# Second branch's attention outputs loaded between the late gates, and two staging tiles for those gates

## The chip, the cores and the metric

The kernel runs on one core of a Trainium2 chip. The metric is device time in microseconds (us) of one execution, the median of several runs. TensorE (PE in the profile) does the matrix products into PSUM, the accumulator memory of eight banks; VectorE (DVE), ScalarE (ACT) and GpSimd (POOL) do the elementwise work; SyncE's queue (SP) issues nearly all DMAs. Every engine works off its own instructions in the order in which they were written, and waits for other engines by semaphores.

## The reference, cut to what matters

One layer over 1040 positions (16 meta tokens and 1024 frames) of width 1024, in float32. Two attention branches of eight heads each share one input projection; their outputs are projected, gated and added:

```python
    log_keep = jnp.where(causal, jax.nn.log_sigmoid(-z), 0.0)
    later = lax.cumsum(log_keep, axis=3, reverse=True) - log_keep
    a = jnp.where(causal, jnp.exp(jax.nn.log_sigmoid(z) + later), 0.0)   # second branch
...
    y_a = _merge_heads(o_a) @ w_o_fox[layer]
    y_b = _merge_heads(o_b) @ w_o_sb[layer]
    mixed = (jax.nn.sigmoid(g_a) * y_a + jax.nn.sigmoid(g_b) * y_b) @ w_out[layer]
```

g_a and g_b, the gates, are 2 x 1024 columns of the input projection. A norm, a residual, a convolutional feed-forward part and a second residual follow; the change doesn't touch them.

## The kernel before, in words

Activations stand with channels on the 128 partitions. Every float32 product is made of three float32r products (a high and a low part of each operand), so 8 blocks of the contraction give 24 matmuls for one output tile (`products`, L133). The 1040 positions are cut in three pieces, `PCS`, of 272, 384 and 384.

Attention goes through 16 heads, x = 0 to 15, branch b = 0 then b = 1. For a head, `attention` walks four chunks c of two query blocks. In the second branch a query block is: scores `s` on PE (L360, L361, L363), two sigmoids on ACT into `kp` and `pr` (L393, L394), a reverse running product `kp` on DVE (L411), a product `pr` on POOL (L412), transposes `tm` and `tr` on PE (L422, L432), casts on ACT and subtractions on DVE that split them into `ptm` and `pt` (L424, L425, L436, L437), and the weighted sum `po` on PE (L426, L442). `ot` and `os` (L445, L447) add its two halves, and a DMA (L448) writes them to `od`, a DRAM tensor for every branch and pair of heads. Between heads `prep(x + 1)` makes the queries, keys and values of the next head (`pq`, `pv`).

`gate(x)` makes one of 16 blocks of 128 gate columns: three tiles `pg` on PE (one for each piece: 24 matmuls 258 wide, twice 24 matmuls 384 wide), in the two PSUM banks of tag "lin"; DVE scales them into a staging tile `gst` in SBUF (L498), where pieces 0 and 1 share one tile and piece 2 has its own; DMAs write the tiles to `gd` in DRAM (L500). Gates 0 to 8 are called inside the loop over the heads, behind the heads of the same numbers. The last seven (`LATE = 7`) are called behind the whole attention stage: the variable x of that loop names gates 9 to 15, whose column blocks i are 12, 5, 13, 6, 14, 7, 15 (a tile `pg120` is block 12, piece 0).

Behind attention comes the output stage: `oraw` tiles (128x258) are loaded from `od` (L571), 32 of them, and split by ACT and DVE into `o` tiles (L572, L573); `gate_load` reads gates back into `gs` and applies the sigmoid; and for eight blocks `y` is multiplied out of them on PE and gated by DVE (L602).

Two things set the order of an engine's work. The program is written in the order told here, and a scheduler with a model of the engines' times orders it by priority as soon as an instruction's operands and its tile's place are to be had. Tiles come from pools. `xp` lives from the start through the late gates. `ga` is opened behind the attention stage, whose pools have then been closed; a tile in a place that an attention tile had waits until that tile's last user is done.

Of the kernel before, what the change touches and what calls it, by code (L numbers as in the profile page):

```python
# [8 lines left out]
F32 = mybir.dt.float32  # L9
F32R = mybir.dt.float32r  # L10
# [6 lines left out]
P = 128  # L17
# [4 lines left out]
L = NM + NX  # L22
A0 = 14
# [21 lines left out]
PCS = [(0, 272), (272, 656), (656, L)]  # L45
QS = [(a, a + QW) for a in range(0, NX, 256)]
# [3 lines left out]
def block_kernel(ctx, tc, xa, xb, wqk, wv, wf, bfg, wg, wo, wout, wup, wdn, gains, conv, cst, out):  # L50
    nc = tc.nc

    def f(ap):
        return ap.bitcast(F32)
# [34 lines left out]
    def sub(eng, dst, a, hi):  # L89
        eng.tensor_tensor(dst, a, f(hi), op=ALU.subtract)  # L90
# [21 lines left out]
    def load_w(src, n, what, eng=None, into=None, hv=False, behind=(None, None)):  # L112
        raw = wp.tile([P, KT * P], F32, tag="wraw", bufs=3, name=f"wr_{what}")
        nc.sync.dma_start(raw[:, :n], src)
        hi, lo = into or (wp.tile([P, KT * P], F32R, tag="whi", name=f"wh_{what}"),
                          wp.tile([P, KT * P], F32R, tag="wlo", name=f"wl_{what}"))
        if hv:
            nc.vector.tensor_copy(hi[:, :n], raw[:, :n])
        else:
            with after(behind[0]):  # L120
                nc.scalar.copy(hi[:, :n], raw[:, :n])  # L121
        with after(behind[1]):
            sub(eng or nc.gpsimd, lo[:, :n], raw[:, :n], hi[:, :n])
        return hi, lo
# [3 lines left out]
    def products(ps, hi, lo, xs, k0, k1, n0, n1, waits=(None,) * 3):  # L128
        xh, xl = xs
        for s, (w, x) in enumerate(((hi, xh), (hi, xl), (lo, xh))):  # L130
            with after(waits[s]):
                for k in range(k0, k1):
                    marks["mm"] = nc.tensor.matmul(  # L133
                        ps,
                        w[:, k * P : (k + 1) * P],
                        x[:, k - k0, n0:n1],
                        start=(k == k0 and s == 0),
                        stop=(k == k1 - 1 and s == 2),
                    )
# [33 lines left out]
    xp = px.enter_context(tc.tile_pool(name="xp", reuse_waits="tile", bufs=1, side="right"))  # L173
    rs1 = xp.tile([P, L], F32, name="rs1")
    with ExitStack() as pa:
# [307 lines left out]
            for h in range(NH):  # L483
                nc.sync.dma_start(od[b][h // 2][(h % 2) * DH : (h % 2 + 1) * DH, 0:2], o[:, h, :])

        def gate(x):
            i = x // 2 + 8 * (x % 2)
            hi, lo = load_w(wg[i], KT * P, f"g{i}")
            for k, (n0, n1) in enumerate(PCS):
                m0 = max(n0, A0)  # L490
                w = n1 - m0
                ps = pl.tile([P, 512], F32, tag="lin", name=f"pg{i}{k}")
                products(ps[:, :w], hi, lo, xs[k], 0, KT, m0 - n0, n1 - n0)
                if k != 1:
                    st = xp.tile([P, PCS[1][1] - A0 if k == 0 else L - PCS[1][1]], F32, tag=f"gst{k}", name=f"gst{i}{k}")
                    a0 = m0
                with tc.high_priority(offset=200):
                    nc.vector.tensor_tensor(st[:, m0 - a0 : n1 - a0], ps[:, :w], rs1[:, m0:n1], op=ALU.mult)  # L498
                if k:
                    nc.sync.dma_start(gd[i][:, a0 - A0 : n1 - A0], st)  # L500

        heads = [(b, h) for b in range(2) for h in range(NH)]
# [33 lines left out]
        for x, (b, h) in enumerate(heads):  # L536
            qk, (vv, vm) = nxt
            attention(b, h, qk, vv, vm)
            if x + 1 == NH:
                psS, psT, psO = psum_pools(2, 3)  # L540
                kpp = side_pool("kpp", 2)
                smask = kpp.tile([P, 2, P], F32R, tag="mask", bufs=1, name="smask")
                raw = apl.tile([P, L], F32, tag="pr", bufs=6, name="smask_raw")[:, :P]
                nc.sync.dma_start(raw, cst[:, CW + P : CW + 2 * P])
                nc.vector.tensor_copy(smask[:, 0, :], ident)
                nc.vector.tensor_copy(smask[:, 1, :], raw)
            if x + 1 < len(heads):
                nxt = prep(x + 1)
            if x < len(heads) - LATE:
                gate(x)  # L550
# [7 lines left out]
    def ftile(j, i, dt, name):  # L558
        return fs[j].tile([P, 4, QW], dt, tag=f"f{i}", name=name)

    with ExitStack() as pb1:
        ga = pb1.enter_context(tc.tile_pool(name="ga", reuse_waits="tile", bufs=2))
        psB = pb1.enter_context(tc.tile_pool(name="psB", reuse_waits="tile", bufs=2, space=PSUM))
        os2 = []
        for q, (n0, n1) in enumerate(QS):
            for b in range(2):
                oh, ol = (ftile(0, 4 * q + 2 * b + s, F32R, f"o{s}{q}{b}") for s in range(2))
                os2.append((oh, ol))
                for kt in range(4):
                    raw = ga.tile([P, QW], F32, tag="oraw", bufs=6, name=f"oraw{q}{b}{kt}")  # L570
                    nc.sync.dma_start(raw, od[b][kt][:, n0:n1])  # L571
                    nc.scalar.copy(oh[:, kt, :], raw)  # L572
                    nc.vector.tensor_tensor(ol[:, kt, :], raw, f(oh[:, kt, :]), op=ALU.subtract)  # L573
        gs2 = {}

        def gate_load(o):
            gs2[o] = [ga.tile([P, NA], F32, tag=f"g{b}", name=f"gs{o}{b}") for b in range(2)]
            for b in range(2):
                nc.sync.dma_start(gs2[o][b], gd[b * 8 + o])
                nc.scalar.activation(gs2[o][b], gs2[o][b], AF.Sigmoid)  # L580

        for o in range(2):
            gate_load(o)
        for x in range(len(heads) - LATE, len(heads)):
            gate(x)
        px.close()
        pc = ctx.enter_context(ExitStack())
        fs.append(pc.enter_context(tc.tile_pool(name="f1", reuse_waits="tile", bufs=1, side="right")))
        ms = [[tuple(ftile(1, 4 * q + 2 * kh + s, F32R, f"m{s}{q}{kh}") for s in range(2)) for kh in range(2)]
              for q in range(4)]  # L590
        for o in range(KT):
            hi, lo = load_w(wo[o], KT * P, f"o{o}", nc.vector)
            if o > 1:
                gate_load(o)
            gs = gs2[o]
            for q, (n0, n1) in enumerate(QS):
                ts = []
                for b in range(2):
                    ps = psB.tile([P, 512], F32, tag=f"y{b}", name=f"y{o}{q}{b}")
                    products(ps[:, :QW], hi, lo, os2[2 * q + b], 4 * b, 4 * b + 4, 0, QW)  # L600
                    ts.append(ga.tile([P, QW], F32, tag=f"t{b}", name=f"t{o}{q}{b}"))
                    nc.vector.tensor_tensor(ts[b], ps[:, :QW], gs[b][:, n0:n1], op=ALU.mult)  # L602
                m = ts[0]
                nc.vector.tensor_tensor(m, m, ts[1], op=ALU.add)
                mh, ml = ms[q][o // 4]
                nc.scalar.copy(mh[:, o % 4, :], m)
                sub(nc.gpsimd, ml[:, o % 4, :], m, mh[:, o % 4, :])
# [260 lines left out]
    for x in range(2 * NPL):  # L868
        k, s = x // 2, x % 2
# [47 lines left out]
    for x in range(2 * 2):  # L917
        k, s = NPL - 2 + x // 2, x % 2
# [187 lines left out]
```

## Time and profile before

| | us |
|---|---|
| three runs | 1681.41, 1680.54, 1678.44 |
| median | 1680.54 |
| the profiled execution | 1680.69, its span 1678.9 |

The span runs from the first to the last instruction in the trace; 1.8 us of the profiled execution lie outside it. "Busy" is the time in which an engine works. A row of waits names who waits for whom, the total, how many times and the longest. PEclk is the TensorE clock granted (1.00 is full). In the timeline "x8" is the number of instructions merged into a row; matmuls overlap, so that a row of eight lasts longer than the distance to the next row.

### The profile page before, as it was taken

What the parts mean: (1) busy time and instruction counts of PE and PEld (TensorE: products, weight loads), DVE (VectorE), ACT (ScalarE), POOL (GpSimd) and SP (SyncE); (2) the same over time, 40 slices, a digit from 0 to 9 for tenths busy, and PEclk for the clock granted to TensorE, in tenths of its full rate; (3) what the DMA queues carried; (4) which work ended last, traced back from release to release, by engine and by line L of the source; (5) the groups of instructions that cost most, each with busy time, mean ns of one, the idle gap of its engine ahead of it and who ended that gap; (6) DMA issues with size and microseconds to landing.
All of it is one profiled execution on the core that took longest, in us unless ns stands there. A gap on an engine that the chain in (4) does not pass through costs nothing.

```text
span 1678.9 us, 29771 instructions
## 1 busy us (share of the span) xinstructions
PE 1636.3 (97%) x11684; PEld 1577.1 (94%) x11684; DVE 1074.4 (64%) x1837; ACT 826.2 (49%) x1708; POOL 434.5 (26%) x306
## 2 busy tenths in 40 slices
PE   7999999999999999999999999999999999999897
PEld 7999999999999999999999999999999999888687
DVE  6456555666678767645536886798888878244522
ACT  6344544444566665544345554566545557333321
POOL 1365655656466565302201000000000000000001
PEclk9999999999999999999999999999999999999999
DMA  4212122212111011264343542333232327344641
GB/s 183 80 56 71 53 63 63 65 47 64 37 47 41 26 45 56 76 203 149 117 139 120 161 170 96 110 112 116 83 105 73 107 77 240 108 149 150 217 126 63
DMA packets 78364, 170.59 MB, mean 102 GB/s; under 512 B 10352, under 2 KB 33648, under 8 KB 78224
## 3 DMA queue, kind: packets, MB, share of 16 engines
q1 hardware_dynamic: 77680, 168.16, 31.4%
q8 instruction: 92, 1.51, 0.4%
q10 hardware_dynamic: 544, 0.52, 0.1%
q14 instruction: 48, 0.39, 0.1%
HBM read 126.43 MB, written 35.77 MB: 97 GB/s over the span
## 4 chain that ended last, share of the span: by engine, by line
PE 86%; DVE 4%; issue 3%; DMA 3%; ACT 2%; POOL 1%; SPq 0%; DVEq 0%; ACTq 0%; POOLq 0%
PE A L812 12%; PE pd L941 12%; PE pq L133 10%; PE pg L133 9%; PE B L812 6%; PE pm L635 6%; PE y L133 5%; PE pu L635 4%; PE pv L133 4%; PE po L442 4%; PE tr L432 3%; PE R L812 3%; PE s L360 2%; PE s L361 2%; DMA gr<-gdr 1%
## 5 line engine op out<-in xcount | busy, mean ns | idle before, releaser
L941 PE MATMUL pd<-g,wh_d 128*128 128x512 f32 x616 | 194.3, 396 | 3.8 <-ACT wh_d L121 3.0
L990 POOL TENSOR_TENSOR acc<-acc,hr 128x512 f32<-128x512 f32 x4 | 5.0, 1273 | 738.7 <-DVE acc L983 738.7
L941 PEld LDWEIGHTS pd<-g,wh_d 128*128 128x128 f32 x616 | 116.7, 190 | 30.8 <-ACT wh_d L121 3.8
L742 DVE SCALAR_TENSOR_TENSOR c<-us,cb,c 128x512 f32<-128x512 f32 x176 | 129.0, 748 | 23.6 <-ACT c L740 22.9
L408 POOL TENSOR_SCALAR pr<-pr,mx 128x144 f32<-128x144 f32 (+3 forms) x64 | 114.0, 1787 | 100.5 <-DVE mx L407 70.2
L437 DVE TENSOR_TENSOR pt<-tr,pt 128x512 fp32r<-128x512 f32 (+1 forms) x160 | 98.5, 632 | 48.1 <-ACT pt L436 46.2
L941 PE MATMUL pd<-g,wl_d 128*128 128x512 f32 x308 | 122.4, 397 | 2.1 <-DVE wl_d L90 2.1
L411 DVE TENSOR_TENSOR_SCAN kp<-kp 128x144 f32<-128x144 f32 (+3 forms) x64 | 101.9, 1601 | 22.7 <-ACT kp L393 21.8
L90 DVE TENSOR_TENSOR wl_d<-wr_d,wh_d 128x896 fp32r<-128x896 f32 (+1 forms) x42 | 47.7, 1137 | 100.8 <-ACT wh_d L121 100.6
L442 PE MATMUL po<-pt,vv 128*128 128x256 f32 (+1 forms) x640 | 110.7, 281 | 1.4 <-DVE pt L437 1.4
L436 ACT CAST pt<-tr 128x512 fp32r<-128x512 f32 (+1 forms) x160 | 83.3, 543 | 44.2 <-PE tr L432 37.3
L412 POOL TENSOR_TENSOR pr<-pr,kp 128x143 f32<-128x143 f32 (+3 forms) x64 | 81.1, 1274 | 92.5 <-DVE kp L411 62.8
L401 ACT ACTIVATE pr<-s,mx 128x144 f32<-128x144 f32 (+6 forms) x112 | 59.9, 540 | 77.4 <-DVE mx L399 54.8
L442 PEld LDWEIGHTS po<-pt,vv 128*128 128x128 f32 x640 | 94.2, 189 | 2.6 <-DVE pt L437 2.2
L121 ACT CAST wh_d<-wr_d 128x896 fp32r<-128x896 f32 (+1 forms) x42 | 41.1, 980 | 105.7 <-PE pd L941 90.5
L432 PE MATMUL tr<-cs,pr 128*128 128x128 f32 x576 | 91.8, 274 | 0.0
L360 PE MATMUL s<-k,q 128*128 128x264 f32 (+9 forms) x240 | 81.0, 339 | 1.1 <-ACT pr L401 0.6
L740 ACT ACTIVATE c<-us,cb 128x512 f32<-128x512 f32 x88 | 71.8, 816 | 15.2 <-DMA gdr<-c 10.4
L133 PE MATMUL pg<-xh,wh_g 128*128 128x384 f32 (+1 forms) x384 | 73.1, 327 | 3.5 <-DVE gst L498 1.6
L133 PE MATMUL pg<-xh,wl_g 128*128 128x384 f32 (+1 forms) x384 | 76.0, 322 | 0.0
L941 PEld LDWEIGHTS pd<-g,wl_d 128*128 128x128 f32 x308 | 58.5, 190 | 16.9 <-DVE wl_d L90 4.2
L133 PE MATMUL y<-o,wh_o 128*128 128x258 f32 x512 | 72.9, 284 | 1.5 <-ACT o L572 1.1
(296 smaller groups left out, 4526.8 us busy)
## 6 DMA issues: line engine op xcount, KB each, us to landing
wu<-in_wup SPq DMA_DIRECT2D x40, 512.0 KB
wr_d<-in_wdn SPq DMA_DIRECT2D x28, 448.0 KB
gdr<-c SPq DMA_DIRECT2D x44, 256.0 KB
gr<-gdr SPq DMA_DIRECT2D x44, 256.0 KB
gs<-gd SPq DMA_DIRECT2D x16, 513.0 KB
wr_g<-in_wg SPq DMA_DIRECT2D x16, 512.0 KB
wr_wo<-in_wout SPq DMA_DIRECT2D x16, 512.0 KB
wr_u<-in_wup SPq DMA_DIRECT2D x16, 512.0 KB
```

The costliest lines, as they stand in the source:

```text
L133: marks["mm"] = nc.tensor.matmul(ps, w[:, k * P : (k + 1) * P], x[:, k - k0, n0:n1], start=(k == k0 and s == 0), stop=(k == k1 - 1 and s = ...
L360: nc.tensor.matmul(ps[:tn, :n], q2[:, t0 : t0 + tn], k1[:, s0:s1], start=True, stop=False)
L408: nc.gpsimd.tensor_scalar(pr[:, :w], pr[:, :w], z, None, op0=ALU.mult)
L411: nc.vector.tensor_tensor_scan(r, r, r, 1.0, op0=ALU.mult, op1=ALU.bypass)
L432: nc.tensor.transpose(tr[:, x * P : (x + 1) * P], prs[tb][:, NM + j * P : NM + (j + 1) * P], ident)
L436: nc.scalar.copy(pt[:, 0, :n], tr[:, :n])
L437: nc.vector.tensor_tensor(pt[:, 1, :n], tr[:, :n], f(pt[:, 0, :n]), op=ALU.subtract)
L442: nc.tensor.matmul(po[:, o0:256], vj, pt[:, s, 256 * j : min(256 * j + 256, n)], start=False, stop=(last and j == 1 and s == 1))
L635: nc.tensor.matmul(ps, (hi, hi, lo)[s][:, c : c + P], xs[kh][s == 1][:, k, :], start=(s == 0 and kh == 0 and k == 0), stop=(s == 2 and kh ...
L742: nc.vector.scalar_tensor_tensor(c, u[:, :, tap : tap + 256], cb[:, x, tap : tap + 1], c, op0=ALU.mult, op1=ALU.add)
L812: nc.tensor.matmul(ps, w[:, (k0 + i) * P : (k0 + i + 1) * P], x[:, i, :], start=(first and s == 0 and i == 0), stop=(s == 2 and i == 3), s ...
L941: nc.tensor.matmul(ps, a[:, (k - k0) * P : (k - k0 + 1) * P], x[:, c0:c1], start=(k == 0 and s == 0), stop=(k == NK - 1 and s == 2))
```

## The change

It has two parts. The staging tiles `gst` of the seven late gates come from pool `ga`, which has two buffers for each tag, in place of `xp`, which has one. And the loads and splits of the attention outputs, one block of 32 ahead of the late gates before, are cut in three: first branch (16 tiles) ahead of them; the first three pairs of heads of the second branch (12 tiles) behind the third late gate, x = 11; the last pair of heads (4 tiles) behind the sixth, x = 14. The number of tiles, matmuls, DMAs and elementwise instructions stays.

```diff
-        def gate(x):
+        def gate(x, stp=xp):
...
                 if k != 1:
-                    st = xp.tile([P, PCS[1][1] - A0 if k == 0 else L - PCS[1][1]], F32, tag=f"gst{k}", name=f"gst{i}{k}")
+                    st = stp.tile([P, PCS[1][1] - A0 if k == 0 else L - PCS[1][1]], F32, tag=f"gst{k}", name=f"gst{i}{k}")
...
-        os2 = []
-        for q, (n0, n1) in enumerate(QS):
-            for b in range(2):
-                oh, ol = (ftile(0, 4 * q + 2 * b + s, F32R, f"o{s}{q}{b}") for s in range(2))
-                os2.append((oh, ol))
-                for kt in range(4):
+        os2 = [tuple(ftile(0, 4 * q + 2 * b + s, F32R, f"o{s}{q}{b}") for s in range(2))
+               for q in range(4) for b in range(2)]
+
+        def heads_out(b, kts):
+
+            for q, (n0, n1) in enumerate(QS):
+                oh, ol = os2[2 * q + b]
+                for kt in kts:
                     raw = ga.tile([P, QW], F32, tag="oraw", bufs=6, name=f"oraw{q}{b}{kt}")
                     nc.sync.dma_start(raw, od[b][kt][:, n0:n1])
                     nc.scalar.copy(oh[:, kt, :], raw)
                     nc.vector.tensor_tensor(ol[:, kt, :], raw, f(oh[:, kt, :]), op=ALU.subtract)
...
+        heads_out(0, range(4))
         for o in range(2):
             gate_load(o)
         for x in range(len(heads) - LATE, len(heads)):
-            gate(x)
+            gate(x, ga)
+            if x == len(heads) - 5:
+                heads_out(1, range(3))
+            if x == len(heads) - 2:
+                heads_out(1, [3])
```

What this makes of the engines' order shows at two places. First PE, at the end of the last head. Before, the rows around its last `po` are these; `pg141` and `pg142` are pieces 1 and 2 of the fifth late gate, `pg70` piece 0 of the sixth:

```order
L432 MATMUL tr1733_8272<-cs_74,pr176_8194 128x128
L432 MATMUL tr1733_8272<-cs_74,pr177_8209 128x128 x2
L133 MATMUL pg141_8845<-xl1_117,wh_g14_8814 128x384 x2
L133 MATMUL pg141_8845<-xh1_116,wl_g14_8815 128x384 x8
L133 MATMUL pg142_8872<-xh2_118,wh_g14_8814 128x384 x4
L442 MATMUL po173_8229<-pt1732_8265,vv13_7474 128x256
L133 MATMUL pg142_8872<-xh2_118,wh_g14_8814 128x384 x4
L133 MATMUL pg142_8872<-xl2_119,wh_g14_8814 128x384
L442 MATMUL po173_8229<-pt1732_8265,vv13_7474 128x256 x3
L442 MATMUL po173_8229<-pt1733_8276,vv13_7474 128x256
L133 MATMUL pg142_8872<-xl2_119,wh_g14_8814 128x384 x3
L442 MATMUL po173_8229<-pt1733_8276,vv13_7474 128x256
```

Now, around the same last `po`; `pg122` is piece 2 of the first late gate, `pg50` piece 0 of the second:

```order
L432 MATMUL tr1733_8272<-cs_74,pr176_8194 128x128
L432 MATMUL tr1733_8272<-cs_74,pr177_8209 128x128 x2
L442 MATMUL po173_8229<-pt1731_8253,vv13_7474 128x256 x3
L442 MATMUL po173_8229<-pt1732_8265,vv13_7474 128x256 x4
L442 MATMUL po173_8229<-pt1733_8276,vv13_7474 128x256 x2
L442 MATMUL po173_8229<-pt1733_8276,vv13_7474 128x128 x2
L133 MATMUL pg122_8456<-xh2_118,wh_g12_8398 128x384 x8
L133 MATMUL pg122_8456<-xl2_119,wh_g12_8398 128x384 x8
L133 MATMUL pg122_8456<-xh2_118,wl_g12_8399 128x384 x8
L133 MATMUL pg50_8490<-xh0_114,wh_g5_8486 128x258 x8
```

Of the late gates only the first two tiles, `pg120` and `pg121`, still stand between the attention's matmuls; 204 matmuls 384 wide and 96 matmuls 258 wide, from `pg122` to the middle of `pg142`, have moved behind the last `po`.

Second, DVE at the same place. Before, where `kp77` is the last running product and `os173` the last output of attention:

```order
L411 SCALAR_TENSOR_TENSOR kp77_8210<-kp77_8210 128x1040
L447 TENSOR_TENSOR os172_8191<-po172_8147,ot172_8189 64x256
L498 TENSOR_TENSOR gst62_8809<-pg62_8784,rs1_113 128x384
L425 TENSOR_TENSOR ptm1_150<-tm173_8230,ptm1_150 16x256
L437 TENSOR_TENSOR pt1730_8241<-tr1730_8236,pt1730_8241 128x512
L437 TENSOR_TENSOR pt1731_8253<-tr1731_8248,pt1731_8253 128x512
L498 TENSOR_TENSOR gst140_8843<-pg140_8818,rs1_113 128x258
L437 TENSOR_TENSOR pt1732_8265<-tr1732_8260,pt1732_8265 128x512
L437 TENSOR_TENSOR pt1733_8276<-tr1733_8272,pt1733_8276 128x384
L498 TENSOR_TENSOR gst140_8843<-pg141_8845,rs1_113 128x384
L447 TENSOR_TENSOR os173_8285<-po173_8229,ot173_8283 64x256
```

Now:

```order
L437 TENSOR_TENSOR pt1732_8265<-tr1732_8260,pt1732_8265 128x512
L437 TENSOR_TENSOR pt1733_8276<-tr1733_8272,pt1733_8276 128x384
L447 TENSOR_TENSOR os173_8285<-po173_8229,ot173_8283 64x256
L498 TENSOR_TENSOR gst120_8427<-pg120_8402,rs1_113 128x258
L498 TENSOR_TENSOR gst120_8427<-pg121_8429,rs1_113 128x384
L575 TENSOR_TENSOR o100_8305<-oraw000_8320,o000_8304 128x258
```

Even the first staging tile, `gst120`, is written behind `os173`. Eleven splits `o` (L575) follow before `gst122`, which empties the bank of `pg122`.

## The prediction

> **What bounds the kernel now.** I read the page's busy shares first, then the stretch of the last two heads in time windows, then who waits there, then the gap behind it.
>
> ```profile
> span 1678.9 us, 29771 instructions
> PE 1636.3 (97%) x11684; PEld 1577.1 (94%) x11684; DVE 1074.4 (64%) x1837; ACT 826.2 (49%) x1708; POOL 434.5 (26%) x306
> ```
>
> PE bounds the whole. A change that leaves PE's matmuls as they are can gain only idle or slowed PE time, and it loses wherever it makes PE idle. So the question is what PE has to do, stretch by stretch, around the moved gates. The projections of the last head end at 625 us (first row below) and the last `po` ends at 719.2; I take the windows from 630 on, two older windows of the same branch for comparison, and in the last row the gates alone (PE, PEld and DVE).
>
> ```profile
> L133 PE MATMUL pq<-xh,wl_qk x360: 283/336/426, 43.5 to 625.1; 128*128 128x384 f32 x120, 128*128 128x272 f32 x60
> ```
>
> ```profile
> core 0: us, PE busy (x) PEld busy (x) DVE busy (x) ACT busy (x) POOL busy (x), PEclk, DMA share, GB/s
> 500.00:520.00 20.00, 18.96 (x135) 17.55 (x133) 18.93 (x25) 13.85 (x37) 10.48 (x8) 1.00 0.04 9
> 560.00:600.00 40.00, 37.72 (x268) 35.93 (x267) 33.55 (x42) 23.93 (x66) 26.69 (x19) 1.00 0.13 38
> 630.00:719.20 89.20, 87.85 (x626) 86.62 (x626) 61.41 (x89) 46.15 (x115) 39.91 (x25) 1.00 0.20 64
> ...
> 630.00:719.20 89.20, 59.03 (x332) 51.93 (x332) 7.00 (x14) 1.00 0.20 64
> ```
>
> From 630 to 719.2 PE idles for 1.35 of 89.2 us, DVE works for 61.41, of which 7.00 are the staging of gates. Attention itself thus costs DVE 54.4 us in this stretch. The 332 gate matmuls have 59.03 us of PE beside them, but matmuls overlap, so that this is no price; the price is the distance from start to start of rows of eight:
>
> ```profile
> 719.74 1.55 PE L133 MATMUL pg<-xh,wl_g 128*128 128x384 f32 x8
> 721.13 1.11 PE L133 MATMUL pg<-xh,wh_g 128*128 128x258 f32 x8
> 722.07 1.11 PE L133 MATMUL pg<-xl,wh_g 128*128 128x258 f32 x8
> ```
>
> Eight take 1.39 us at 384 and 0.94 at 258, or 174 and 118 ns each. By the order, 228 of the 332 are 384 wide and 104 are 258 wide: 39.7 + 12.3 = 52 of the 89.2 us. The late gates are what PE does while attention's chain through ACT, DVE and POOL is under way. Who waits in this stretch:
>
> ```profile
> POOL pr L412 <- DVE kp L411: 21.6, 7, 6.5
> ACT ot L445 <- PE po L442: 12.4, 8, 4.2
> ACT pt L436 <- PE tr L432: 10.8, 8, 3.3
> DVE pt L437 <- ACT pt L436: 9.7, 13, 2.7
> DVE kp L411 <- ACT kp L393: 4.7, 5, 2.2
> ```
>
> All the others wait for each other; PE is not among them, since it always has a gate to go on with.
>
> **The change, part by part.** *The gates leave attention.* By the new order, 204 matmuls of 384 and 96 of 258 move behind the last `po`: 204 x 0.174 + 96 x 0.118 = 46.7 us of PE work. If attention went on as slowly as now, all of it would be added. If attention shrank by as much, nothing would. It would then have to run from 630 to its end in 89.2 - 46.7 = 42.5 us, which is less than the 54.4 us that DVE alone needs for it. The staging's 7.00 us are already taken off there. So this part loses at least 54.4 - 42.5 = 11.9 us, if DVE never waits.
>
> It will wait. The end of the chain overlaps with nothing:
>
> ```profile
> 701.81 2.32 DVE L411 TENSOR_TENSOR_SCAN kp<-kp 128x1040 f32<-128x1040 f32 x1
> 704.30 2.03 POOL L412 TENSOR_TENSOR pr<-pr,kp 128x1039 f32<-128x1039 f32 x1 [6.47 <-DVE kp L411]
> 708.29 0.82 PE L432 MATMUL tr<-cs,pr 128*128 128x128 f32 x6
> 708.82 1.08 ACT L436 CAST pt<-tr 128x512 fp32r<-128x512 f32 x2
> 709.44 1.29 DVE L437 TENSOR_TENSOR pt<-tr,pt 128x512 fp32r<-128x512 f32 x2
> 719.20 0.37 ACT L445 COPY ot<-po 64x256 f32<-64x256 f32 x1 [4.24 <-PE po L442]
> 719.60 0.42 DVE L447 TENSOR_TENSOR os<-po,ot 64x256 f32<-64x256 f32 x1 [2.83 <-ACT ot L445]
> ```
>
> The last running product ends at 704.13. POOL's product needs 2.2 us from there, six transposes 0.8, the first casts 0.9, four subtractions at 0.65 another 2.6, and the last `po` about 1: some 8 us, where 15 pass today with gates in between. DVE has about 3.4 us to do in them. The remaining 51.0 us it does at the share that it reaches where attention is what holds things up: 33.55 / 40 = 84% from 560 to 600, 18.93 / 20 = 95% from 500 to 520 (in both, PE has idle time, so that gates or projections were not the limit). That makes 51.0 / 0.95 + 8 = 62 to 51.0 / 0.84 + 8 = 69 us. I take 90%, between the two: 51.0 / 0.90 + 8 = 65 us. The loss is 65 - 42.5 = **22.5 us**.
>
> *The gap behind attention.* The output stage has waits today:
>
> ```profile
> 743.85 1.29 PE L133 MATMUL y<-o,wh_o 128*128 128x258 f32 x7 [1.09 <-ACT o L572]
> 746.67 0.39 PE L133 MATMUL y<-o,wh_o 128*128 128x258 f32 x1 [0.29 <-DVE o L573]
> 748.53 0.56 DVE L498 TENSOR_TENSOR gst<-pg,rs 128x384 f32<-128x384 f32 x1 [1.92 <-DMA gd<-gst]
> 749.15 2.82 PE L133 MATMUL pg<-xh,wh_g 128*128 128x384 f32 x8 [1.61 <-DVE gst L498]
> ...
> 748.00:750.00 2.00, 0.85 (x3) 0.85 (x4) 1.23 (x3) 0.00 (x0) 0.00 (x0) 0.82 0.97 343
> 750.00:752.00 2.00, 2.00 (x8) 2.00 (x7) 0.01 (x1) 0.46 (x2) 0.00 (x0) 0.50 0.68 241
> 752.00:754.00 2.00, 2.00 (x11) 2.00 (x11) 1.09 (x3) 0.96 (x3) 0.00 (x0) 0.82 0.02 8
> ```
>
> PE waits 1.09 + 0.29 us for the splits of `oraw`, and 1.61 us for a staging tile whose write to DRAM hasn't landed: 3.0 us. Then it runs at a granted clock of 0.50 to 0.82 for some 4 us and loses about 1.5 more. Both go. With some 71 us of gates behind attention (the 46.7, and 12 matmuls and two gates that stood there before) the 32 splits are done long before `y` needs them, and the second buffer of `gst` takes the DMA out of the way. Nothing is late in their place: DVE, ACT and POOL have next to nothing else there. That is **-4.5 us**, all that the change can gain.
>
> *The restart.* Behind the last `po` PE finds both "lin" banks full, with `pg120` and `pg121`, and can't begin `pg122` before DVE has emptied the first. DVE comes to it behind `ot` 0.37, `os` 0.42 and its own 0.42 us, with hand-offs **1.7 us**. Two tiles later PE wants the bank of `pg122`, and DVE empties that behind eleven splits.
>
> ```profile
> 720.60 6.53 SPq L571 DMA_DIRECT2D oraw<-od  x11
> 723.50 0.76 ACT L572 CAST o<-oraw 128x258 fp32r<-128x258 f32 x2 [2.52 <-DMA oraw<-od]
> 723.95 0.43 DVE L573 TENSOR_TENSOR o<-oraw,o 128x258 fp32r<-128x258 f32 x1 [2.06 <-ACT o L572]
> ```
>
> From the first load issued to the first subtraction pass 3.4 us, and eleven at 0.43 make 4.7. With 0.9 us for `os` ahead of the load and 0.6 for the bank, `pg122` is emptied 9.6 us behind the last `po`; PE arrives at 1.7 + 4.2 + 2.8 = 8.7. It waits **0.9 us**, between 0 and 2. After so much idling I expect the restart to run slowed, like the stretch from 749 on: **1.5 us**, between 0 and 3.
>
> *What costs nothing.* The 14 `gst` move with the gates, to an idle DVE. The casts of gate weights (ACT, first row) and their low parts (POOL, second row) go along:
>
> ```profile
> L121 ACT CAST wh_g<-wr_g 128x1024 fp32r<-128x1024 f32 x4 | 4.2, 1045 | 2.1 <-PE pg L133 2.1
> 706.71 2.38 POOL L90 TENSOR_TENSOR wl_g<-wr_g,wh_g 128x1024 fp32r<-128x1024 f32 x1 [0.38 <-issue]
> ```
>
> They are 1.0 and 2.4 us a gate, against 24 x 0.118 + 48 x 0.174 = 11.2 us of its matmuls. SP passes the 12 + 4 later loads between gates; of a gate's weights those of five late gates are issued before attention ends, and the sixth (block 7) needs to be there only 4.2 + 4 x 11.2 = 49 us after it. If that load came 10 us late it would still cost nothing.
>
> **Sum.** 22.5 - 4.5 + 1.7 + 0.9 + 1.5 = +22.1 us, on the profiled execution's 1680.69 (0.15 above the median of 1680.54): 1702.8, say **1703 us**.
>
> [...]
>
> **The rivals.** *DVE fills the tail (A).* With nothing in front of its matmuls, attention comes close to DVE's own 54.4 us: say 57 us. +14.5 - 4.5 + 1.7 gives +11.7, or 1692 us. The 95% window speaks for it, the end of the chain against it.
>
> *A slow tail (B).* Attention's own PE work in the stretch is 87.85 - 52 = 36 us. If PE's idling brings the clock down to 0.50 for most of the tail, that becomes 72 us and PE bounds its own tail again, each transposition and score making the chain longer: 75 to 80 us, +32.5 to +37.5, with the other terms -0.4: 1713 to 1718 us. The clock at 750 speaks for it. [...]
>
> *Not slower (C).* The two waits go (-4.5) and the gates cost nothing. That needs a tail of 41 to 45 us; it decides at 42.5 + 4.5 - 1.7 = 45.3. DVE's 54.4 us speak against it, and so do the 42 us that ACT has (46.15 less 4.2 for gate weights). It could only be if DVE's running products got much shorter without gates beside them. 1676 to 1681 us.
>
> **Chances.** My forecast, a tail of 59 to 72 us, 0.62; A, 0.14; B, 0.20; C, 0.04. What a measurement of this kernel can tell from no change is about 0.2%, or 3.4 us; of C one half is faster, one half within it. So faster 0.02, same 0.02, slower 0.96. The range is from A's value to B's upper end, 1692 to 1718 us; it leaves out C, the faster half of A, and tails beyond 80 us.
>
> **What would show it.** Right: PE's busy time from 630 to the last `po` falls to about 60%, and `po` ends near 695; DVE's share there is 80 to 90%; a block of gates follows without a gap above 2 us, some 71 us long; no wait of `y` for `o`, and none for `gst` behind a DMA. The output stage ends some 22 us later than today, where the last row of `y` is
>
> ```profile
> L133 PE MATMUL y<-o,wl_o x256: 276/283/293, 736.1 to 842.0; 128*128 128x258 f32 x128
> ```
>
> Wrong would be: a clock below 0.8 over the tail (B); a tail under 59 us (A); or a PE that waits in the block of gates, for weights or loads, which I priced at 0.9 us.

## The result, and the profile after

| | before, us | after, us |
|---|---|---|
| median (4 runs each) | 1680.97 | 1703.33 |
| lowest to highest | 1678.44 to 1683.64 | 1701.02 to 1704.41 |
| the profiled execution | 1680.69 | 1701.02 |

The ratio after to before is 1.0146, with a 95% interval of 1.0133 to 1.016: slower by 22.4 us in the medians, by 20.3 us between the two profiled executions. The forecast was 1703 us. It came out close because two errors of some 5 us each went opposite ways, as the accounting below shows.

The head of the page after: the busy time of DVE, ACT and POOL is within 1.4 us of what it was, and PE's is 9.0 us longer though it has the same 11684 matmuls (the last section says why that isn't 9.0 us more of work).

```profile
span 1699.2 us, 29767 instructions
PE 1645.3 (97%) x11684; PEld 1583.2 (93%) x11684; DVE 1075.7 (63%) x1837; ACT 826.5 (49%) x1708; POOL 433.1 (25%) x306
```

Three tiles mark the stages: the projections of the last head, the last `po`, and the end of the output stage.

```profile
L133 PE MATMUL pq<-xh,wl_qk x360: 283/336/426, 44.5 to 626.1; 128*128 128x384 f32 x120, 128*128 128x272 f32 x60
L442 PE MATMUL po<-pt,vv x640: 218/281/562, 95.4 to 690.8; 128*128 128x256 f32 x160
L133 PE MATMUL y<-o,wl_o x256: 277/283/293, 772.9 to 864.6; 128*128 128x258 f32 x128
```

Up to the last head the trace of after runs 1.0 us later than that of before (626.1 against 625.1), so its 631.0 stands for the prediction's 630. Attention ends 28 us earlier than before (691 against 719), and the output stage ends 22.6 us later (864.6 against 842.0). The time was lost between these two marks. In windows (the tail of attention; its part up to the last running product; one stretch inside it; the first gates behind it; and a stretch of these):

```profile
core 0: us, PE busy (x) PEld busy (x) DVE busy (x) ACT busy (x) POOL busy (x), PEclk, DMA share, GB/s
631.00:691.10 60.10, 48.48 (x325) 43.08 (x324) 52.07 (x75) 41.57 (x110) 28.77 (x21) 0.94 0.08 19
631.00:682.00 51.00, 40.68 (x279) 36.09 (x278) 46.73 (x66) 38.70 (x104) 26.75 (x20) 0.97 0.08 20
660.00:670.00 10.00, 8.44 (x59) 8.41 (x59) 9.70 (x24) 7.45 (x21) 4.18 (x5) 0.83 0.05 14
691.00:720.00 29.00, 23.84 (x128) 23.52 (x127) 14.92 (x29) 15.18 (x31) 4.74 (x2) 0.82 0.77 239
700.00:710.00 10.00, 6.08 (x26) 5.88 (x25) 6.02 (x11) 6.17 (x12) 2.35 (x1) 0.68 0.88 264
```

In the tail DVE works for 52.07 of 60.1 us, 87%: it is the engine that holds attention up, where before PE was full (87.85 of 89.2 us). In 29 us behind the tail PE idles for 5 us and has a granted clock of 0.82. Who waits, from 620 to 870, the three longest of PE's rows:

```profile
PE pg L133 <- DVE gst L498: 5.2, 2, 3.9
PE po L426 <- DVE os L447: 4.4, 3, 2.2
PE po L426 <- DVE ptm L425: 1.6, 3, 1.2
```

PE now waits for DVE's part of attention (`os`, `ptm`), and twice, for 5.2 us in all, for the staging of gates. Of the waits that stood in the gap before, `y` for the splits of `o` and `gst` for its DMA, none is left in the rows of PE and DVE up to 870. The two waits of 5.2 us, in order of time:

```profile
689.71 0.67 PE L442 MATMUL po<-pt,vv 128*128 128x256 f32 x4
690.57 0.55 PE L442 MATMUL po<-pt,vv 128*128 128x256 f32 x3 [0.19 <-DVE pt L437]
692.36 2.08 PE L133 MATMUL pg<-xh,wh_g 128*128 128x384 f32 x8 [1.24 <-DVE gst L498]
694.24 2.73 PE L133 MATMUL pg<-xl,wh_g 128*128 128x384 f32 x8
696.80 1.56 PE L133 MATMUL pg<-xh,wl_g 128*128 128x384 f32 x8
698.20 1.11 PE L133 MATMUL pg<-xh,wh_g 128*128 128x258 f32 x8
...
705.12 2.93 PE L133 MATMUL pg<-xh,wh_g 128*128 128x384 f32 x8 [3.92 <-DVE gst L498]
707.84 2.76 PE L133 MATMUL pg<-xl,wh_g 128*128 128x384 f32 x8
710.40 1.62 PE L133 MATMUL pg<-xh,wl_g 128*128 128x384 f32 x8
```

The first wait is the restart. The tile at 692.36 is `pg122`; its 24 matmuls fill 5.84 us up to the next tile at 698.20, against 4.17 (3 x 1.39) at full clock. The wait of 3.92 us at 705.12 is for the bank that `pg122` had: it is emptied behind the eleven splits, as foreseen, but the last of these splits took 2.37 us where one takes 0.43. DVE and POOL at that moment:

```profile
701.97 2.35 POOL L90 TENSOR_TENSOR wl_g<-wr_g,wh_g 128x1024 fp32r<-128x1024 f32 x1 [17.18 <-ACT wh_g L121]
```

```profile
702.23 2.37 DVE L575 TENSOR_TENSOR o<-oraw,o 128x258 fp32r<-128x258 f32 x1 [0.83 <-ACT o L574]
704.52 0.55 DVE L498 TENSOR_TENSOR gst<-pg,rs 128x384 f32<-128x384 f32 x1
```

### The profile page after: what moved, and what is told of

Its sections match the earlier page's. It is cut to its first block, busy times and chain, and to the rows that moved or that the text cites. A ratio compares the mean times of both kernels' runs of the same rounds, so it can differ in the third digit from the quotient of the medians.

```text
span 1699.2 us, 29767 instructions
## 1 busy us (share of the span) xinstructions
PE 1645.3 (97%) x11684; PEld 1583.2 (93%) x11684; DVE 1075.7 (63%) x1837; ACT 826.5 (49%) x1708; POOL 433.1 (25%) x306
## 4 chain that ended last, share of the span: by engine, by line
PE 85%; DVE 5%; DMA 4%; ACT 3%; issue 2%; POOL 1%; SPq 0%; DVEq 0%; ACTq 0%; POOLq 0%
PE A L820 12%; PE pd L949 12%; PE pq L133 10%; PE pg L133 9%; PE B L820 6%; PE pm L643 5%; PE y L133 5%; PE pu L643 4%; PE pv L133 4%; PE po L442 4%; PE R L820 3%; PE tr L432 3%; DVE kp L411 2%; PE s L360 2%; PE s L361 2%
## 5 line engine op out<-in xcount | busy, mean ns | idle before, releaser
L133 PE MATMUL pq<-xh,wl_qk 128*128 128x272 f32 (+1 forms) x360 | 73.4, 326 | 0.0
```

The lines of the kernel that those rows point to most:

```text
L133: marks["mm"] = nc.tensor.matmul(ps, w[:, k * P : (k + 1) * P], x[:, k - k0, n0:n1], start=(k == k0 and s == 0), stop=(k == k1 - 1 and s = ...
```

## The experiments

The theory: the staging tiles in `ga` take the late gates out of attention, since a place in `ga` becomes free only when attention's tiles are done. That reason is read from the program and from DVE's order, where the first `gst120` stands behind `os173`. The last two heads then go at DVE's pace with PE partly idle, and the same 46.7 us of gates come afterwards. Experiments 1 to 4 ran on one chip (before 1678.29 us there, the median of 29 runs), 5 to 8 on another (before 1677.04, 11 runs). The change itself was not timed again on these two; what is compared across chips is the ratio to before.

### 1. The later loads alone

The changed kernel with the late gates' staging left in `xp`, as before:

```diff
         for x in range(len(heads) - LATE, len(heads)):
-            gate(x, ga)
+            gate(x)
```

> The loads between the gates as in the change, the staging tiles of all gates in the long-lived pool with one buffer as before. Theory (the place of the staging tiles drives the gates out of attention, and that alone costs): gates stand in the tail of attention again, 1678 to 1682 us against 1681 before and 1703 after. Rival (the loads between the gates hold up the gates' own DMAs and DVE): 1690 us or more.

Measured: 1678.63 us (11 runs), ratio 1.0002 [0.9993, 1.001]. The tail's window and PE's waits for `y`:

```profile
631.00:691.10 60.10, 58.75 (x423) 57.70 (x422) 46.07 (x67) 33.80 (x86) 31.56 (x21) 1.00 0.19 59
```

```profile
PE y L133 <- ACT o L574: 1.1, 2, 0.9
PE y L133 <- DVE t L610: 0.6, 1, 0.6
```

PE has its gates in the tail again, 423 matmuls in the stretch against 325. Cutting the loads in three by itself costs nothing and gains nothing that the interval could tell.

### 2. The staging alone

The late gates' staging in `ga`, and all 32 loads in one block ahead of the gates, in the order of before (the calls at the end; `gate` takes the pool as an argument, as in the change):

```diff
         for x in range(len(heads) - LATE, len(heads)):
-            gate(x)
+            gate(x, ga)
```

> The staging tiles in the later pool with two buffers as in the change, all 32 attention outputs loaded ahead of the late gates as before. Theory: the same tail of about 60 us and the same loss, 1702 to 1707 us, the upper part if more splits stand in front of the first stagings. Rival (the loads cost): 1681 us.

Measured: 1700.92 us (4 runs), ratio 1.0134 [1.012, 1.0147], an interval that overlaps the change's own. The absolute time is just below the range expected; on this chip before was 2.7 us faster too. The tail and the wait in the gates are the change's, nearly to the digit:

```profile
631.00:691.10 60.10, 48.36 (x325) 42.86 (x323) 52.05 (x75) 41.21 (x109) 28.64 (x21) 0.94 0.08 19
```

```profile
PE pg L133 <- DVE gst L498: 5.2, 2, 4.0
```

The loss thus comes with the staging alone; within the intervals the moved loads add nothing to it. The staging differs from before in two things, the pool and the number of buffers, and no run separates them: two buffers in `xp` were not tried. That it is the place and not the second buffer is argued from the program's order, not shown by a run.

### 3. Two staging tiles for the last two gates only

Before, with the two gates that stood behind attention anyway staged in `ga` (loads as in experiment 2):

```diff
         for x in range(len(heads) - LATE, len(heads)):
-            gate(x)
+            gate(x, ga if x >= len(heads) - 2 else xp)
```

> Only the last two gates, which run behind attention before as well, stage in the later pool with two buffers; five keep the long-lived pool; all loads ahead of the late gates as before. Theory (the wait of 1.6 us for a staging tile and the slow clock behind it are a loss of their own, apart from the tail): 1677 to 1680 us. Rival A (any staging in the later pool drives gates out of attention): 1690 us or more. Rival B (the waits for the splits take the place of the staging wait): 1680 to 1682 us.

Measured: 1676.65 us (12 runs), ratio 0.9989 [0.9978, 1.0], the best of all versions, by about 0.1% and at the edge of what can be told. The wait of a gate for its staging tile is gone; what is left of PE's waits from 700 to 870 is

```profile
PE y L133 <- ACT o L575: 0.8, 1, 0.8
PE y L133 <- DVE t L607: 0.3, 1, 0.3
PE y L133 <- DVE o L576: 0.2, 1, 0.2
```

### 4. The same with the change's later loads

Of the change, the staging of its first five late gates put back into `xp`:

```diff
         for x in range(len(heads) - LATE, len(heads)):
-            gate(x, ga)
+            gate(x, ga if x >= len(heads) - 2 else xp)
```

> As the kernel with the last two gates in the later pool, and the loads between the gates as in the change. Theory: gates cover attention and both waits of the output stage are gone, 1676 to 1679 us, under the kernel before by 2 to 4.5 us. Rival (the later loads of the second branch now come too late for the output stage, since only 24 us of gates are left behind attention): 1680 to 1685 us.

Measured: 1679.84 us (12 runs), ratio 1.001 [1.0, 1.0021]; this interval and that of experiment 3 touch at 1.0. The time lies just below the rival's range and just above the theory's, but its mechanism is the rival's: with the gates back inside attention only the last gate stands behind the last loads, and the output stage runs into them. ACT waits for the load; PE waits first for DVE's `t`, which stands in DVE's order behind splits that wait for ACT, and then for ACT itself:

```profile
749.51 1.12 ACT L574 CAST o<-oraw 128x258 fp32r<-128x258 f32 x3 [4.38 <-DMA oraw<-od]
```

```profile
751.49 1.23 PE L133 MATMUL y<-o,wh_o 128*128 128x258 f32 x8 [2.77 <-DVE t L610]
...
755.78 2.30 PE L133 MATMUL y<-o,wh_o 128*128 128x258 f32 x9 [2.54 <-ACT o L574]
```

So the later loads take away what experiment 3 had gained (3.2 us between the two medians). In the change this doesn't show: all but two tiles of its late gates run behind attention, and its `y` waits for no `o`. Nor do later loads with the gates inside attention always cost: experiment 1 has them too, at the time of before, with waits of `y` of 1.7 us in all against 5.3 here. Where this difference comes from was not followed up.

### 5. The first branch's splits behind the second late gate

Of the change, to take the eleven splits out of the way of `pg122`'s bank:

```diff
-        heads_out(0, range(4))
         for o in range(2):
             gate_load(o)
         for x in range(len(heads) - LATE, len(heads)):
             gate(x, ga)
+            if x == len(heads) - LATE + 1:
+                heads_out(0, range(4))
```

> The change, with the first branch's 16 loads and splits behind the second late gate instead of ahead of the first, so that the third staging stands ahead of the splits on DVE. Theory (3.9 us of wait behind the splits and some 2.6 us of slow clock behind that wait are a part of the loss of their own): the wait goes, ratio to before 1.008 to 1.011 instead of 1.0134 to 1.0146. Rival (the next banks wait behind splits in its place): 1.0125 to 1.0145.

Measured: 1700.62 us (4 runs), ratio 1.0136 [1.012, 1.0152], not separate from the change's. PE's sum of waits for staging and the rows of the restart and of its longest wait:

```profile
PE pg L133 <- DVE gst L498: 7.8, 6, 3.2
```

```profile
692.25 1.66 PE L133 MATMUL pg<-xh,wh_g 128*128 128x384 f32 x8 [1.24 <-DVE gst L498]
...
706.92 1.65 PE L133 MATMUL pg<-xh,wh_g 128*128 128x384 f32 x8 [3.24 <-DVE gst L498]
```

```profile
691.00:720.00 29.00, 22.12 (x139) 21.30 (x139) 13.96 (x29) 15.27 (x31) 4.77 (x2) 1.00 0.78 236
```

The rival was right: the wait moved to another tile, and the sum of waits grew from 5.2 to 7.8 us; where the splits stand, a later bank waits for them. The granted clock is another matter. Here the restart, after the same wait of 1.24 us, runs at full clock. Ahead of it, from 631 to 691.1, the granted clock is 0.91 here and 0.94 in the change.

### 6. and 7. 48 useless DVE instructions in the last two heads, in the change and in the kernel before

In both kernels three multiplications of 128x128, whose result nobody uses, behind each running product of heads 14 and 15:

```diff
                 nc.vector.tensor_tensor_scan(r, r, r, 1.0, op0=ALU.mult, op1=ALU.bypass)
+                if 8 * b + h >= 14:
+                    for n in range(3):
+                        nc.vector.tensor_tensor(dum, kp[:, 0:128], rs1[:, 0:128], op=ALU.mult)
```

> The change, with 48 additional DVE multiplications of 128x128 behind the running products of the last two heads, in the kernel's sense useless; some 0.25 to 0.3 us each, 12 to 14 us in all. Theory (without gates the tail is DVE's): nearly all of it lands on the time, 9 to 14 us over the change, 1710 to 1716 us. Rival (the tail is set by the chain through ACT, POOL and a slow PE): 0 to 5 us over the change.

> The kernel before, with the same 48 additional DVE multiplications. Theory (PE bounds the tail while gates fill it, and DVE idles for 28 of 89 us): 0 to 4 us over the kernel before. Rival (the tail is DVE's there too): 9 us or more.

Measured in the change: 1713.48 us (4 runs), ratio 1.0216 [1.02, 1.0231]. That is 36.4 us over before, where the change is 22.4 over it: the additions cost some 14 us, and 12.9 against experiment 5 on the same chip, which has the plain change's tail. Measured in before: 1684.15 us (6 runs), ratio 1.0038 [1.0024, 1.0051], +7.1 us, between theory and rival. The 48 instructions, first in the change (from 620 to 710; the columns are those of DVE alone), then in before:

```profile
620.00:710.00 90.00, 26.48 (x48) 0.87 0.07 18
```

```profile
620.00:720.00 100.00, 37.93 (x48) 1.00 0.17 53
```

They took 26.5 and 37.9 us, some two and nearly three times what 48 would take at their median of 0.29 us, since some were held up; the row is that of the second run:

```profile
L415 DVE TENSOR_TENSOR dum<-kp,rs x48: 254/294/2372, 633.4 to 715.1; 128x128 f32<-128x128 f32 x48
```

In before, 37.9 us more of DVE's time cost 7.1; the other 31 fell into time in which DVE had waited while PE went on with gates. In the change 26.5 us cost 13 to 14. This agrees with DVE setting the pace in the tail of the change, though not for every microsecond, since the additions also fill its waits (97% busy there now, second row below, against 87%). It is no clean price: PE's waits for POOL's product also rose, from 0.5 to 4.0 us, so that a part of the loss may have come by way of POOL. The first row shows DVE nearly full in before as well, at full clock and with PE at 55.31 of 60.1 us:

```profile
631.00:691.10 60.10, 55.31 (x381) 52.84 (x380) 58.99 (x98) 31.17 (x78) 27.45 (x19) 1.00 0.16 52
```

```profile
631.00:691.10 60.10, 44.77 (x262) 38.43 (x261) 58.42 (x104) 35.27 (x93) 23.66 (x19) 0.86 0.06 14
```

### 8. The late gates' weights: low parts on DVE in place of POOL

Of the change, to take POOL's 2.35 us away from beside the splits:

```diff
-            hi, lo = load_w(wg[i], KT * P, f"g{i}")
+            hi, lo = load_w(wg[i], KT * P, f"g{i}", nc.gpsimd if stp is xp else nc.vector)
```

> The change, with the low parts of the seven late gates' weights made by DVE (about 1.2 us each) instead of POOL; on DVE they stand behind the third staging. Theory (a split that took 2.37 us instead of 0.43 was held up by POOL's subtraction of the same time): all splits ahead of the third staging take 0.41 to 0.45 us, PE's longest wait there falls from 3.9 to about 2 us; time within 4 us of the change, since two low parts of 1.2 us fall into the DVE-bound tail. Rival (the long split waited for its load): the longest wait stays near 3.9 us.

Measured: 1698.0 us (4 runs), ratio 1.0124 [1.0107, 1.014]; the interval overlaps the change's, so that no gain is shown in the time. In the trace the split that had taken 2.37 us takes 0.43, and PE's wait behind it 1.85 us, 2.07 less:

```profile
701.87 0.43 DVE L575 TENSOR_TENSOR o<-oraw,o 128x258 fp32r<-128x258 f32 x1 [0.82 <-ACT o L574]
```

```profile
702.82 2.66 PE L133 MATMUL pg<-xh,wh_g 128*128 128x384 f32 x8 [1.85 <-DVE gst L498]
```

That POOL's subtraction stretched the split, and the split the wait, is thereby shown: the rival, a late load, would have left both as they were.

## Why the prediction was right, and where by luck

| term | predicted, us | in the trace after, us |
|---|---|---|
| tail of attention against 42.5 | 65 - 42.5 = 22.5 | 60.1 - 42.5 = 17.6 |
| gap behind attention | -4.5 | -4.5 (taken over: none of its waits is left) |
| restart | 1.7 | 1.24 |
| wait behind eleven splits | 0.9 | 3.92 |
| slowed clock at the restart | 1.5 | 4.2 |
| sum | 22.1 | 22.5 |

*That the gates leave attention and are lost as cover* was right: experiment 2 has all of it with the staging alone, and experiment 1 none of it with the loads alone. That DVE sets the tail is borne out by its 87%, by PE's longest waits there (`os`, `ptm`) and, with the reserve made there, by experiments 6 and 7. One reading was not quite right: from 630 on PE was not free of waits before, it waited 1.4 us for DVE's `qkt`, which is the whole of its 1.35 us of idling; the wait is the same after.

*The size of the tail* was the first term off, 4.9 us too long. Up to the last running product's end DVE had some 47.3 us of work and not 51.0 (46.73 up to 682.0 in the windows, and the rest of this row), and did it in 51.6 us, 92% and not 90%. The end of the chain took 8.5 us against the 8 predicted:

```profile
679.98 2.62 DVE L411 TENSOR_TENSOR_SCAN kp<-kp 128x1040 f32<-128x1040 f32 x1
```

Most of the error is thus the amount of DVE's work ahead of the chain's end; its share was nearly right. Of the whole tail DVE's work is 52.07 us where the prediction had 54.4, for the same 75 instructions: the small operations on the meta tokens (`smini` L455 and L470, `mx` L477) took 3.4 us instead of 6.2, and the running products of 912 and 1040 columns 1.2 us more. What made them shorter and longer was not tested. The rest is work that lay in the end of the chain (52.07 - 47.3 = 4.8 us where I had put 3.4).

*The wait behind the splits* was the second, 3.0 us too short and beyond its own bounds of 0 to 2. Its place and its cause were right; the step that failed is "eleven at 0.43", which left out that a split can stand beside POOL's subtraction of gate weights. I had put that subtraction under what costs nothing. Experiment 8 gives 2.07 us of the wait to it.

*The slowed clock* was the third, 4.2 us where 0 to 3 had been allowed: `pg122` took 1.67 us too long, and `pg51` behind the second wait 2.57 (6.74 us from its start at 705.12 to the next tile's at 711.86, against 4.17). I had counted one slow restart; there were two.

*The gap* was right in sign, and rather too small: all of its waits are gone from PE's list, and the granted clock is 1.00 from 720 to 866. What it had cost can be estimated from starts before: from 742.35 to 753.60 PE began 24 matmuls at 258 and 16 at 384, some 5.6 us of slots in 11.25 us, so about 5.6 us and not 4.5. Experiment 3, which removes the staging wait alone, is 1.6 us faster in the median, about that wait's 1.61, though its interval reaches to no gain.

The sum stands at 22.5 us by the trace, 21.6 by the later end of `y` less the 1.0 that was there before the last head; a gap of 5.6 in place of 4.5 would account for it, to 0.2 us. At the end of `y` after lies 22.6 us behind before, and still 22.6 at the first `pd`, a product of the feed-forward part (1433.4 against 1410.8); at the end of the span it is 20.3. So 2.3 us are won back from `pd` on, which the change doesn't touch: PE's waits there for its weights are, before and after,

```profile
PE pd L941 <- ACT wh_d L121: 3.0, 2, 2.0
```

```profile
PE pd L949 <- ACT wh_d L121: 1.7, 1, 1.7
```

and the granted clock in the 40 us around these waits is 0.91 before (1540 to 1580) and 0.96 after (1562.6 to 1602.6). The 2.3 us lie within the scatter of the runs.

Several of the signs that I named came out otherwise. PE's busy share in the tail was 81% (48.48 of 60.1) and not 60%, partly since the tail was shorter, partly for a reason given in the last section. `po` ended at 691, not 695, the same error as the tail's. And the block of gates had a gap above 2 us, the 3.92, which I had named as a sign of being wrong, and lasted 79.8 us (692.36 to 772.17), not 71. Rival A, DVE filling the tail at 57 us, was nearer than I thought: the tail's 60.1 lies between it and the forecast. Rival B, a slow tail, is ruled out by the clock of 0.94.

## What to carry to other kernels

Work that fills an engine's idle time is only worth what it covers, and as this program is scheduled a buffer's pool can decide when it runs: the staging tiles from a pool opened behind the running stage came into use only when that stage was done (argued from the order; no run moved the place alone). Before giving such work more buffers, look at which pool they come from, and give them only to the part that stood behind the stage anyway (experiment 3). Where a sum comes out right, compare it with the trace term by term: here a tail that was 4.9 us too long hid waits and a clock that were 5.3 us too short.

## What the runs showed of the hardware

A DVE split beside a POOL subtraction took longer and ended shortly behind it: the 128x258 split in the change, begun 0.26 us behind POOL's 2.35 us, took 2.37 us instead of 0.43 and ended 0.28 us behind it, and took again 0.43 when POOL's work had moved away (experiment 8); in experiment 5 a split of the same size, begun 0.54 us behind a POOL subtraction of 2.40 us, took 2.15 and ended 0.29 us behind it.

The granted clock fell to 0.83 from 660 to 670 in the tail, where no wait of PE is above 2.2 us, and to 0.68 from 700 to 710, around a wait of 3.92 us. These are means. In windows of 2 us (660 to 668, 680 to 712) the clock is halved for a stretch and then full again: 0.85, 0.50, 0.80 and 1.00 from 692 to 700 in the change, which makes 0.6 + 2 + 0.8 = 3.4 us at half clock; the three windows from 748 on that the prediction shows give 3.4 us as well, and 702 to 712, with 0.91, 0.50, 0.50, 0.50 and 0.88, twice as much. Nearly the same tail and the same wait of 1.24 us led to a slow restart in the change (1.67 us lost; 0.82 from 691 to 720) and to one at full clock in experiment 5 (1.00 from 691 to 720), where the tail ahead of it had 0.91 against 0.94. The four stretches in the change begin, by these windows, at about 662.7, 683.2, 693.4 and 703.6 us, which is 20.5, 10.2 and 10.2 us apart, six and three times 3.4; whether more than chance is in that, four starts don't show. What starts one isn't settled by these runs; that idling does, as the forecast of a slowed restart took it, is not shown by them either.

PE's busy time is no share of its capacity here. With the same 11684 matmuls it grew by 9.0 us, a part of it by matmuls at half clock (0.50 from 704 to 710). By the prediction's working, attention's own matmuls fill 36 us of slots and the two gate tiles left in the tail 52 - 46.7 = 5.3: together, as an estimate, 69% of the 60.1 us, or 73% at a clock of 0.94. Yet PE counts as busy for 81%. A `po` matmul is recorded with 0.28 us (its median above), while in a dense row of eight at 258 one takes up 0.118; where matmuls stand apart, the busy time counts more than the slots.
